# The second block's attention: the second pass of a score product over 128 rows in place of 64

## The chip, the cores and the metric

One core of a Trainium2 chip runs the whole program in one launch. The metric is the device time of that launch in microseconds (us), the median of several runs; smaller is better. The engines in the profile are PE (TensorE, with PEld for its weight loads), DVE (VectorE), ACT (ScalarE), POOL (GpSimd) and SP (SyncE), which here only issues DMAs.

## The reference, cut to what matters

The model is two blocks one behind the other, each of two layers, on 512 tokens of 1024 features in float32. The change lies in the second block's windowed attention: 16 query heads of 64 features, 4 heads of keys and values, each serving four query heads, in blocks of 128 tokens that see the block before, their own and the one behind.

```python
def windowed_gqa(q, k, v, rel_bias, sink):
    ...
    scores = jnp.einsum("bnqhgd,bnkhd->bhgnqk", qb, kb,
                        preferred_element_type=jnp.float32) * (HEAD_DIM ** -0.5)
    ...
    scores = jnp.where(valid, scores + bias, NEG_INF_2)
    sink_l = sink.astype(jnp.float32).reshape(N_KV_HEADS, G, 1, 1, 1)
    m = jnp.maximum(jnp.max(scores, axis=-1, keepdims=True), sink_l)
    p = jnp.exp(scores - m)
    denom = jnp.sum(p, axis=-1, keepdims=True) + jnp.exp(sink_l - m)
    p = (p / denom).astype(v.dtype)
    out = jnp.einsum("bhgnqk,bnkhd->bnqhgd", p, vb)
```

Beside it stand a convolution along the tokens, a pooling branch, gates, an output projection and a feed-forward part, as projections of 1024 (or 2816) features.

## The kernel before, in words

**Products in parts.** Every float32 value that goes through PE is split in a rounded part (`hi`, type float32r) and the rest (`lo`), so that two float32r tiles sum to it exactly. A projection is made of three passes for each 128 x 128 tile of weights (`mm3`, L259 to L261): `hi` by `hi`, `hi` by `lo`, `lo` by `hi`, all over 128 rows and mostly 512 columns, adding in one PSUM bank.

**Scores.** Queries and keys have 64 features, and the array has 128 rows. So `q_split` (L1280, L1281) puts both parts of a head's query on the 128 rows of one tile: for an even head the rounded part on rows 0 to 63 and the rest on rows 64 to 127, for an odd head the other way round. `k_evac` (L1261 to L1264) makes for each key head two tiles: one that holds the rounded part in both halves, and one that holds the rest in both halves (the second half of it is a copy by POOL, L1264). The product of a head and a block of 128 queries (`scores`) is then two passes in one bank: L1321 takes all 128 rows of the query against the rounded keys (both query parts by `hi`), L1322 the 64 rows with the query's rounded part against the keys' rests. The keys seen are 256 for the first and last block and 384 for the two between, so the passes have 256 or 384 columns. There are 16 heads x 4 blocks x 2 layers = 128 such products.

**What follows a product.** VectorE adds the bias and takes the maximum (L1324), forms the shift (L1328), ScalarE takes the exponential with its sum (L1329). When a head's four blocks are done, `scale` (L1338 to L1342, VectorE) divides by the sums, `turn` transposes 128 x 128 pieces on PE (L1352) and copies them out (L1355, VectorE and ScalarE in turns), `mix` multiplies them with the values (L1367, 64 columns of the array for each of two heads) and ScalarE copies the result out (L1370). PSUM has 8 banks, given out in turn.

**Order.** PE's order is fixed when the program is built. `weave` puts three streams together: the pairs' scores and scales (`sc`, 8 pairs of heads per layer), their turns and mixes (`tm`), and as filling the convolution branch's projections (`fill`, L1381 to L1396 on the other engines). An item has a cost (109 per 128 columns for a product) and due times behind the items that it needs, and the scores of a pair are spaced by 900 of the planner's units. The other engines' instructions are issued in the same order, with weights' splits (L1657, L1658) three chunks ahead. The bias of each pair is loaded by POOL's queue (L627) a pair ahead.

Of the kernel before, what the change touches and what calls it, by code (L numbers as in the profile page):

```python
# [49 lines left out]
# first block  # L50
# [11 lines left out]
# second block  # L62
# [6 lines left out]
# t5 bucket boundaries: bucket b begins at distance BOUND[b]  # L69
# [8 lines left out]
def shape_constants():  # L78
    """Constants that depend on the shapes alone."""
    hot1 = np.zeros((33, NT1), np.float32)  # L80
    for n in range(N0):
        j = 255 - n
        hot1[np.searchsorted(BOUND1, j, side="right") - 1 if 0 <= j <= 128 else 32, n] = 1.0
    for n in range(N1):
        j = 127 - n
        hot1[np.searchsorted(BOUND1, 4 * j, side="right") - 1 if j >= 0 else 32, N0 + n] = 1.0
        ok = j >= 0 and j % 4 == 0
        hot1[np.searchsorted(BOUND1, 4 * j, side="right") - 1 if ok else 32, N0 + N1 + n] = 1.0
    hot2 = np.zeros((33, NT2), np.float32)
    for n in range(NT2):  # L90
        rel = n - 255
        b = np.searchsorted(BOUND2, abs(rel), side="right") - 1 + (16 if rel > 0 else 0)
        hot2[b if abs(rel) <= 128 else 32, n] = 1.0
    # causal mask behind three blocks of zeros, edges of the pooling windows, rope's rows
    mask = np.zeros((P, 4 * P), np.float32)
    mask[:, 3 * P:] = np.where(np.arange(P)[None, :] <= np.arange(P)[:, None], 0.0, NEG)
    edge = np.ones((4, 16), np.float32)
    for g, w in enumerate(POOL_W):
        for t in range(w // 2):
            edge[g, t] = w / (t + w // 2)  # L100
        for t in range(S - w // 2 + 1, S):
            edge[g, 16 - (S - t)] = w / (S - t + w // 2)
    edge = np.broadcast_to(edge.reshape(1, 64), (P, 64))
    inv = (1.0 / np.power(np.float32(10000.0), np.arange(0, 32, 2, dtype=np.float32) / np.float32(32))).astype(np.float32)
    # rope's rows: 32 with the first halves of two heads, 32 with the second ones, and again for two more heads
    row = np.arange(P)
    freq = np.tile(inv, 8).reshape(P, 1)
    sign = np.where(row % 64 < 32, 1.0, -1.0).reshape(P, 1)
    parity = np.stack([row % 32 < 16, row % 32 >= 16], axis=1)
    small = np.ascontiguousarray(np.concatenate([mask, edge, freq, sign, parity], axis=1), np.float32)  # L110
    return np.concatenate([hot1, hot2], axis=1), small


class Weight:
    """One tile of weights, [128, n] as the host lays it out; split on the chip, or given to `use`."""
# [5 lines left out]
class Item:  # L121
    """A stretch of the tensor engine's work, with what follows from it on the other engines.

    after: items, each with the time that its results take to be ready behind it.
    """
# [14 lines left out]
class Order:  # L140
    """The tensor engine's order: streams of items woven so that what an item needs is ready."""
# [16 lines left out]
    def weave(self, *streams, hold=0):  # L158
        """The last stream is kept back by `hold`, to have some of it for the others' end."""
        total = [sum(i.cost for i in x) or 1 for x in streams]  # L160
        at, done = [0] * len(streams), [0.0] * (len(streams) - 1) + [float(hold)]
# [28 lines left out]
class Kernel:  # L190
# [31 lines left out]
    def held(self, n, dt=F32, tag=None):  # L222
        """A tile that the first block holds, or one of the second in its place."""
# [7 lines left out]
    def split(self, y, shift=None, factor=None):  # L231
        """y (+ shift, or * factor) as the sum of two float32r tiles: exact."""
        nc = self.nc
# [12 lines left out]
    def splits(self, ys):  # L246
        """Some tiles' splits, the engines taking turns."""
# [15 lines left out]
    def proj(self, get, cols, K, x, evac, m=P, step=8, grain=2, part=slice(0, S)):  # L263
        """Items for evac(W[:, cols].T @ X), X's tiles given by x() on use; or of X's columns `part`."""
# [20 lines left out]
    def proj_rows(self, get, cols, n, K, x, evac, step, blocks=(0, 1, 2, 3)):  # L285
        """Items for evac(i, (X.T @ W[:, cols])[rows of block i]); x() gives, by block, X's tiles."""
# [23 lines left out]
    def proj_wide(self, get, cols, x, evacs, part=slice(0, S), box=None):  # L310
        """Four projections at once, an item for every two of X's tiles; or the second of two parts, with the first's box."""
# [30 lines left out]
    def row_sums(self, acc, m=4):  # L342
        """Sums over the features, [token of block j, j]."""
# [5 lines left out]
    def root(self, ps, n, by=None, m=4):  # L349
        """1 / sqrt(mean + eps) of each token, the sums taken by a factor squared."""  # L350
# [9 lines left out]
        # a Newton step, as the table's root is short of float32  # L360
# [13 lines left out]
    def spread(self, dg, out=None):  # L374
        """The diagonals on all partitions."""
# [8 lines left out]
    def half_norm_items(self, l, half):  # L384
        """The first block's norm of half of the tokens: three items, then four for two feature tiles each."""
# [34 lines left out]
    def norm_items(self, acc, n, key):  # L420
        """Items that leave the tokens' factors under key, from the squares under acc."""
# [15 lines left out]
    def two_norms_items(self):  # L437
        """The same for a norm behind a norm: under r1 the first's factors, under r those of both."""
# [16 lines left out]
    def warm_sqrt(self, _):  # L455
        """The root's table, ahead of its use."""
# [8 lines left out]
    def setup(self):  # L465
        """What the first norm needs, and small constants."""
        nc, ap, st = self.nc, self.ap, self.st
        # silu(c) on all partitions, the first layer's input
# [15 lines left out]
        # keys of the first block; in the second, rows with zeros around the tokens and the pooling's partial sums  # L484
# [12 lines left out]
    def sigmoid2(self, ps):  # L497
        """tanh(x / 2), one short of twice the sigmoid: of the exponential's table."""
# [4 lines left out]
    def gated(self, out, s, y):  # L503
        """y by twice the sigmoid."""
        self.nc.vector.scalar_tensor_tensor(out, s, 1.0, y, ALU.add, ALU.mult)

    def warm(self, n):
        """Products of zeros: the array's clock stays up where it would wait for loads."""
# [27 lines left out]
    def setup_rope(self, _):  # L536
        """cos and the signed sin, for angles of any size."""
# [26 lines left out]
    def turned(self, ps, n):  # L564
        """Rows of rope, n of them, as the two terms of their sum."""
# [23 lines left out]
    def bias_tables(self, _):  # L589
        """Relative-position biases by distance, with masked distances in a row of their own."""  # L590
# [7 lines left out]
        # each table in 128 rows, to be read with a shift of one from row to row  # L598
# [11 lines left out]
    def load_bias1(self, hp):  # L610
        """[q, (head, g0's 256 keys | g1's 128 | g2's 128)] of two heads; g0's rows in order (t % 4, t // 4)."""
# [19 lines left out]
    def ada_weights(self, l):  # L631
# [3 lines left out]
        def use(raw, j):  # L635
            junk = self.t(BF16, [P, D])
            if l == 0 and j % 2 == 1 and j < 8:
                # beside the others, while there are many at once
# [12 lines left out]
    def ada_finish(self, l, ks):  # L651
        """Shift and scale of the feature tiles ks."""
# [17 lines left out]
    def first_layer(self, l):  # L670
# [20 lines left out]
        # -- latents and the shared rope key  # L691
# [15 lines left out]
        def kr_rope(_):  # L707
# [3 lines left out]
            # the keys' other parity is zero, as the rows of queries hold two heads  # L711
# [16 lines left out]
        # -- dilated: values  # L728
# [15 lines left out]
        # -- dilated: queries and keys of two heads  # L744
# [25 lines left out]
        # -- dilated attention of two heads  # L770
# [37 lines left out]
        # the groups' maxima and sums by token: g0's rows are (t % 4, t // 4) of block b, those of g1 and g2 t // 4 for t % 4  # L808
# [95 lines left out]
        else:  # L904
            # the first half of the tokens is ready, the second follows
# [62 lines left out]
    def first_rest(self, l, sc, tm, fill):  # L968
# [7 lines left out]
        # -- the dilated branch's way out  # L976
# [15 lines left out]
        # -- latent attention  # L992
# [88 lines left out]
        # what of it does not wait for the dilated branch's values goes beside that branch's end  # L1081
# [44 lines left out]
        # keys and queries of pair j + 2 take the places of those of pair j  # L1126
# [6 lines left out]
        # -- the latent branch's way out, the gates and the output projection  # L1133
# [20 lines left out]
        def x_load(_):  # L1154
            gate = self.mod[l][:, 16:24]
            # half of it, as what it gates is doubled
# [8 lines left out]
        def wo_evac(ps, f):  # L1165
            x = st["xr"][f]
            nc.vector.scalar_tensor_tensor(x, ps, self.mod[l][:, 16 + f:17 + f], x, ALU.mult, ALU.add)
            # the last norm's gains, and the next norm's, ahead of the tokens' factors
# [7 lines left out]
        def wo_half(ps, f, half):  # L1176
# [6 lines left out]
            # the squares one tile behind, so that they wait for nothing  # L1183
# [13 lines left out]
        if l + 1 < DEPTH:  # L1197
            # by halves of the tokens, so that the next norm of the first goes beside the second
# [14 lines left out]
    def ahead(self, x, gname, l, f):  # L1213
        """x with the next norm's gains, short of the tokens' factors."""
# [5 lines left out]
    def second_layer(self, l):  # L1220
# [8 lines left out]
        def norm(gname, wide, more):  # L1229
            """The norm's items, woven with those of a wide projection and others that go ahead of it."""  # L1230
# [21 lines left out]
        # -- keys (twice, for heads in the upper and the lower rows) and values  # L1252
        def k_evac(ps, i):
            # of each head the first part twice, [hi; hi], and the rest twice
# [20 lines left out]
        def q_split(y, j, scale):  # L1275
            """Of each head both parts on the 128 rows; the first where its keys are."""
# [20 lines left out]
        # -- attention  # L1297
# [3 lines left out]
        def scores(h, b):  # L1301
            j, h2 = h // 2, h % 2

            def fn(_):
# [12 lines left out]
                rs = slice(64 * h2, 64 * h2 + 64)  # L1317
# [4 lines left out]
                nc.tensor.matmul(ps[:, :n], lhsT=q[rs, qs], rhs=lo[rs, ks], start=False, stop=True)  # L1322
# [55 lines left out]
        # -- convolution along the tokens  # L1378
# [53 lines left out]
        # -- the branches' ways out, each with its gate  # L1432
# [100 lines left out]
        # -- feed-forward, in two halves of its width  # L1533
# [85 lines left out]
    def emit(self, items, chunks):  # L1619
        """Issue the items, with the weights' loads and splits ahead of them."""  # L1620
# [10 lines left out]
        def load(c):  # L1631
            off, ws = chunks[c]
            n = sum(w.n for w in ws)
            # the first loads have the places of later tiles too
# [41 lines left out]
# per-feature columns: name -> (first column, columns)  # L1676
# [64 lines left out]
```

## Time and profile before

| | |
|---|---|
| median of 3 runs | 3356.23 us (3355.78 to 3357.96) |
| profiled execution: span from its first to its last instruction | 3356.0 us; the profile shows no time outside it |
| PE busy | 3303.6 us, 98% |
| DVE, ACT, POOL busy | 54%, 38%, 12% |
| chain that ended last, by engine | PE 88%, DVE 4%, issue 3%, ACT 2% |
| DMA | 101 GB/s on average |

The table is read from the top: how long, who is busy, who is on the chain. A matmul's duration in this profile is longer than the time it takes from the stream (ends are modelled, and matmuls overlap), so the distance from one start to the next is what counts on PE. Times in a timeline are us from the start of the span.

### The profile page before, as it was taken

Reading aid. Unit: us, or ns where it says so; the run is one execution under the profiler, and the core shown is the slowest. Engines: PE = TensorE matmul, PEld = TensorE weight load, DVE = VectorE, ACT = ScalarE, POOL = GpSimd, SP = SyncE. Lnnn points to the kernel's source line nnn. Section 1 sums busy time; section 2 is a strip of 40 time slices with the busy share of each in tenths; the row PEclk is TensorE's granted clock in tenths of the full one; section 3 lists DMA queues with packets and bytes.
Section 4 is the critical chain, followed back from the end, with each engine's and each line's share of the span. In section 5 each row is a group of like instructions: output and inputs, shape, how many; then the busy total and the mean of one; then the engine's idle time right before and its main releaser. Section 6 shows DMA issues by size and latency. Waiting matters only on the chain.

```text
span 3356.0 us, 40708 instructions
## 1 busy us (share of the span) xinstructions
PE 3303.6 (98%) x15484; PEld 2625.9 (78%) x15488; DVE 1798.3 (54%) x3659; ACT 1275.2 (38%) x2432; POOL 396.9 (12%) x651
## 2 busy tenths in 40 slices
PE   8999999999999999999999999999999999999998
PEld 5878767799778677877688878888876788888886
DVE  7556776465446765576544555333666525463333
ACT  3344344343444443454433333223444423242222
POOL 3033301020122010200004110000000014000000
PEclk8999999999999999999999999999999999999999
DMA  6454531263221122332222332232322223322322
GB/s 221 138 160 150 124 88 67 82 214 126 82 70 56 53 74 76 124 115 77 73 88 80 109 113 101 88 104 82 127 90 71 70 89 99 125 88 91 110 89 69
DMA packets 104979, 340.20 MB, mean 101 GB/s; under 512 B 14116, under 2 KB 17236, under 8 KB 104784
## 3 DMA queue, kind: packets, MB, share of 16 engines
q1 hardware_dynamic: 94320, 309.90, 27.4%
q0 software_dynamic: 10464, 27.72, 3.3%
q8 instruction: 121, 1.98, 0.2%
q14 instruction: 74, 0.61, 0.1%
HBM read 329.04 MB, written 16.35 MB: 103 GB/s over the span
## 4 chain that ended last, share of the span: by engine, by line
PE 88%; DVE 4%; issue 3%; ACT 2%; DMA 1%; POOL 1%; DVEq 0%; SPq 0%; ACTq 0%; POOLq 0%
PE ps L259 25%; PE ps L260 24%; PE ps L261 24%; PE ps L1034 2%; PE ps L1322 1%; PE ps L1367 1%; PE ps L1352 1%; PE ps L1072 1%; PE ps L302 1%; PE ps L303 1%; PE ps L304 1%; PE ps L1059 1%; DMA rows<-dt 1%; PE ps L888 1%; PE ps L790 1%
## 5 line engine op out<-in xcount | busy, mean ns | idle before, releaser
L259 PE MATMUL ps<-t,hi 128*128 128x512 f32 (+1 forms) x3904 | 1553.2, 398 | 6.8 <-ACT t L239 3.9
L260 PE MATMUL ps<-t,hi 128*128 128x512 f32 (+1 forms) x3904 | 1504.2, 385 | 0.9 <-DVE t L240 0.7
L261 PE MATMUL ps<-t,lo 128*128 128x512 f32 (+1 forms) x3904 | 1503.7, 385 | 0.0
L1658 DVE TENSOR_TENSOR lo<-raw,hi 128x1024 fp32r<-128x1024 f32 (+5 forms) x562 | 666.5, 1188 | 732.9 <-ACT hi L1657 732.4
L259 PEld LDWEIGHTS ps<-t,hi 128*128 128x128 f32 x3904 | 735.0, 188 | 184.9 <-issue 20.3
L261 PEld LDWEIGHTS ps<-t,lo 128*128 128x128 f32 x3904 | 735.1, 188 | 148.3
L260 PEld LDWEIGHTS ps<-t,hi 128*128 128x128 f32 x3904 | 735.9, 189 | 145.3 <-issue 6.7
L1657 ACT CAST hi<-raw 128x1024 fp32r<-128x1024 f32 (+6 forms) x566 | 551.5, 977 | 238.4 <-PE ps L260 156.3
L239 ACT CAST t<-t 128x512 fp32r<-128x512 f32 x154 | 91.0, 619 | 376.6 <-DVE t L1559 174.6
L240 DVE TENSOR_TENSOR t<-t,t 128x512 fp32r<-128x512 f32 x154 | 106.7, 716 | 105.9 <-ACT t L239 105.9
L805 ACT ACTIVATE p<-p,sm 128x128 f32<-128x128 f32 (+1 forms) x192 | 80.1, 418 | 142.7 <-DVE sm L802 142.6
L1329 ACT ACTIVATE p<-p,sm 128x256 f32<-128x256 f32 (+1 forms) x128 | 72.1, 563 | 162.1 <-DVE sm L1328 161.1
L1040 ACT ACTIVATE p<-p,sm 128x128 f32<-128x128 f32 (+3 forms) x128 | 71.9, 562 | 157.8 <-DVE sm L1039 156.8
L302 PE MATMUL ps<-hi,t 128*128 128x512 f32 (+1 forms) x272 | 105.2, 387 | 12.2 <-ACT t L242 11.7
L303 PE MATMUL ps<-hi,t 128*128 128x512 f32 (+1 forms) x272 | 102.6, 377 | 0.6 <-DVE t L243 0.6
L304 PE MATMUL ps<-lo,t 128*128 128x512 f32 (+1 forms) x272 | 101.7, 374 | 0.0
L1435 ACT ACTIVATE t<-ps 128x512 f32<-128x512 f32 x48 | 28.7, 598 | 171.3 <-PE ps L261 171.3
L1462 POOL TENSOR_TENSOR c<-c 128x527 f32<-128x527 f32 (+3 forms) x40 | 51.8, 1294 | 346.1 <-ACT c L1458 344.1
L1034 PE MATMUL ps<-c,t 128*128 128x128 f32 (+3 forms) x256 | 89.7, 439 | 0.4 <-DVE t L999 0.4
L1002 POOL TENSOR_TENSOR t<-t,t 64x512 f32<-64x512 f32 x32 | 42.3, 1336 | 358.6 <-DVE t L571 237.2
L302 PEld LDWEIGHTS ps<-hi,t 128*128 128x128 f32 x272 | 68.0, 250 | 19.4 <-ACT t L242 14.1
L1559 DVE TENSOR_TENSOR t<-ps,t 128x512 f32<-128x512 f32 x38 | 26.3, 692 | 101.4 <-PE ps L261 101.4
(229 smaller groups left out, 2850.1 us busy)
## 6 DMA issues: line engine op xcount, KB each, us to landing
raw<-in_w_dram SPq DMA_DIRECT2D x512, 512.0 KB, 3.3
raw<-in_w_dram SPq DMA_DIRECT2D x32, 384.0 KB, 3.0
raw<-in_w_dram SPq DMA_DIRECT2D x32, 320.0 KB, 2.8
xd<-t SPq DMA_DIRECT2D x24, 256.0 KB, 4.8
t<-xd POOLq DMA_DIRECT2D x24, 256.0 KB, 5.3
bias<-rows POOLq DMA_DIRECT2D x32, 192.0 KB, 2.8
rows<-dt POOLq DMA_DIRECT2D x1, 4088.0 KB, 38.8
raw<-in_w_dram SPq DMA_DIRECT2D x10, 256.0 KB, 2.6
```

The costliest lines, as they stand in the source:

```text
L239: nc.scalar.copy(hi, y)
L240: nc.vector.tensor_tensor(lo, y, hi.bitcast(F32), ALU.subtract)
L259: mm(out, lhsT=w[0], rhs=x[0], start=start, stop=False)
L260: mm(out, lhsT=w[0], rhs=x[1], start=False, stop=False)
L261: mm(out, lhsT=w[1], rhs=x[0], start=False, stop=stop)
L302: mm(ps, lhsT=xh, rhs=hi[:, s], start=k == 0, stop=False)
L303: mm(ps, lhsT=xl, rhs=hi[:, s], start=False, stop=False)
L304: mm(ps, lhsT=xh, rhs=lo[:, s], start=False, stop=k == kt - 1)
L805: nc.scalar.activation(pr[:, s], pr[:, s], AF.Exp, bias=nm[:, g, h2, b:b + 1], accum_out=ml[:, 1, g, h2, b:b + 1])
L1034: nc.tensor.matmul(ps[:, :n], lhsT=st["q", h][:, b * P:(b + 1) * P], rhs=self.kh[h % 4][:, :n], start=True, stop=True)
L1657: nc.scalar.copy(hi[:, :n], src[:, :n])
L1658: (nc.gpsimd if chunks[c][1][0].aside else nc.vector).tensor_tensor(lo[:, :n], src[:, :n], hi[:, :n].bitcast(F32), ALU.subtract)
```

## The change

The second pass takes all 128 rows: both parts of the query against the keys' rests, which lie on both halves. The result gets one term more, rest by rest. The slice of rows is dropped; the number, order and planned cost of the instructions stay. The other lines of the diff only take comments and docstrings out, one line for one line, so that line numbers behind the dropped slice are smaller by one.

```diff
@@ -1314,12 +1314,11 @@
                 pr, sm = st["p", h], st["st", h]
                 n = (HI[b] - LO[b]) * P
                 o = 384 * h2 + (LO[b] - b + 1) * P
-                rs = slice(64 * h2, 64 * h2 + 64)
                 ps = self.ps()
                 q, (hi, lo) = st["q", h], st["k", h // 4]
                 qs, ks = slice(b * P, (b + 1) * P), slice(LO[b] * P, HI[b] * P)
                 nc.tensor.matmul(ps[:, :n], lhsT=q[:, qs], rhs=hi[:, ks], start=True, stop=False)
-                nc.tensor.matmul(ps[:, :n], lhsT=q[rs, qs], rhs=lo[rs, ks], start=False, stop=True)
+                nc.tensor.matmul(ps[:, :n], lhsT=q[:, qs], rhs=lo[:, ks], start=False, stop=True)
```

## Rows read from the trace of the kernel before

**Rows 1.** The page's part 1: busy us, share of the span, instructions.

```profile
PE 3303.6 (98%) x15484; PEld 2625.9 (78%) x15488; DVE 1798.3 (54%) x3659; ACT 1275.2 (38%) x2432; POOL 396.9 (12%) x651
```

**Rows 2.** Stretches, both layers' attention: length, busy PE, PEld, DVE, ACT, POOL, clock, DMA.

```profile
1450.00:1691.00 241.00, 241.00 (x1095) 169.85 (x1094) 151.01 (x400) 107.30 (x244) 7.52 (x14) 1.00 0.26 87
2419.00:2660.00 241.00, 241.00 (x1095) 169.88 (x1094) 150.77 (x400) 107.52 (x244) 6.44 (x12) 1.00 0.25 84
```

**Rows 3.** The chain that ended last, from 1447 to 1690, by line.

```profile
by line: PE ps L259 26.8%; PE ps L261 21.8%; PE ps L260 21.7%; PE ps L1322 9.0%; PE ps L1352 8.4%; PE ps L1367 8.3%; PE ps L1321 4.1%
```

**Rows 4.** Line L1322: durations in ns, forms; idle before it (us, times).

```profile
L1322 PE MATMUL ps<-held,t x96: 379/410/444, 1451.2 to 2585.4; 64*128 64x256 f32 x48, 64*128 64x384 f32 x48
...
L1322 PE MATMUL ps<-t,t x32: 379/410/443, 1622.9 to 2645.5; 64*128 64x256 f32 x16, 64*128 64x384 f32 x16
...
  issue: 27.8, 106
```

**Rows 5.** Timeline around the first product: start, length, engine, line, [idle before].

```profile
1450.33 0.39 PE L259 MATMUL ps<-t,hi 128*128 128x512 f32 x1
1450.33 0.19 PEld L260 LDWEIGHTS ps<-t,hi 128*128 128x128 f32 x1
1450.56 0.39 PE L260 MATMUL ps<-t,hi 128*128 128x512 f32 x1
...
1451.01 0.28 PE L1321 MATMUL ps<-t,t 128*128 128x256 f32 x1
...
1451.21 0.18 PEld L1322 LDWEIGHTS ps<-held,t 64*128 64x128 f32 x1 [0.24 <-issue]
1451.21 0.38 PE L1322 MATMUL ps<-held,t 64*128 64x256 f32 x1
...
1451.52 0.50 PE L259 MATMUL ps<-t,hi 128*128 128x512 f32 x1
...
1451.86 0.40 PE L260 MATMUL ps<-t,hi 128*128 128x512 f32 x1
```

**Rows 6.** Timeline of passes over 128 rows and 256 columns.

```profile
1439.74 0.28 PE L302 MATMUL ps<-hi,t 128*128 128x256 f32 x1
1439.86 0.28 PE L303 MATMUL ps<-hi,t 128*128 128x256 f32 x1
```

**Rows 7.** Timeline, a product over 384 columns and the second pass behind it.

```profile
1455.02 0.33 PE L1321 MATMUL ps<-t,t 128*128 128x384 f32 x1
...
1455.99 0.40 PE L260 MATMUL ps<-t,hi 128*128 128x512 f32 x1
```

**Rows 8.** Timeline, a product that a mix follows.

```profile
1520.80 0.38 PE L1322 MATMUL ps<-held,t 64*128 64x256 f32 x1
...
1521.11 0.65 PE L1367 MATMUL ps<-t,t 128*64 128x256 f32 x4
```

**Rows 9.** Timeline of POOL, the last of the keys' copies.

```profile
1433.03 0.61 POOL L1264 CAST t<-t 64x512 fp32r<-64x512 f32 x1 [0.74 <-DVE t L1262]
```

**Rows 10.** Timeline, from the first product to the first turn, both layers.

```profile
1461.14 0.42 DVE L1324 CUSTOM_DVE_ANT_0 p<-ps,bias 128x256 f32<-128x256 f32 x1
...
1477.17 1.28 DVE L1342 TENSOR_SCALAR p<-p,sm 128x256 f32<-128x256 f32 x4
...
1478.41 0.33 PE L1321 MATMUL ps<-t,t 128*128 128x384 f32 x1
...
1480.53 0.38 PE L1352 MATMUL ps<-c,p 128*128 128x128 f32 x2
...
2445.76 1.28 DVE L1342 TENSOR_SCALAR p<-p,sm 128x256 f32<-128x256 f32 x4
...
2449.31 0.39 PE L1352 MATMUL ps<-c,p 128*128 128x128 f32 x2
```

**Rows 11.** Waits from 1450 to 1691: us in total, times, longest.

```profile
DVE t L1355 <- PE ps L1352: 14.3, 13, 3.2
...
DVE p L1324 <- PE ps L1322: 12.1, 11, 2.8
```

## The prediction

> **What bounds the kernel now.** I read first the page's busy shares [rows 1]: the tensor engine is busy for 98% of the span, VectorE, the next, for 54%. A busy tensor engine may still hold bubbles, as the ends of its matmuls are modelled, so the second view is the table of stretches, for the two stretches in which the second block's attention runs, one per layer [rows 2]: in 241 us each PE has no idle time, the weight loads fill 170 us, VectorE 151 us, ScalarE 107 us, and the granted clock is 1.00, the upper level of 2.4 GHz. The chain inside the first of them [rows 3] is PE alone, and the pass that the change touches, L1322, holds 9.0% of it although it does little of the work. So here the end is set by how soon one matmul may start behind the other, and start-to-start times are to be read, not durations. The third view is that line's own summary [rows 4]: 96 and 32, so 128 second passes, half over 256 and half over 384 columns; 27.8 us of idle time stand before them in 106 cases under "issue", which means that nothing the profile shows was awaited. The fourth is the timeline around one score product.
>
> **What one score product costs.** Among full passes, L260 starts 0.23 us behind L259, and its load (all 128 rows) begins while L259 streams [rows 5]. With 256 columns, passes over 128 rows follow each other at 0.12 us, each with weights of its own [rows 6]. The score product over 256 columns departs from that: from L1321 at 1451.01 to the 64-row L1322 it takes 0.20, from there to the next projection's L259 0.31, and from that to L260 0.34, though L259 has 512 columns like any other; 0.85 in all [rows 5]. L1322's load comes after 0.24 of idle time and starts with its matmul, where L260's ran ahead of it. So going to the 64 rows costs about 0.1 and coming back about 0.3, at two places: before L259, and behind it. With 384 columns, it is 0.97 from L1321 to L260 [rows 7].
>
> **The change part by part.** Nothing is added or removed in count: one matmul with one weight load stays one, in the same place of the order; the planner's costs (109 per 128 columns) are untouched, so no DMA, split or evacuation moves in any queue. The stationary and the moving side of the second pass grow from 64 to 128 rows, of tiles that are whole already.
>
> *The second pass.* As a 128-row pass of the same type as L1321 it should stand in the stream like any other. 256 columns: 0.12 + 0.12 + 0.23 = 0.47 in place of 0.85, which saves 0.38. For 384 columns the trace has no such pass in a stream; it lies between the spacing of 256 (0.12) and of 512 columns (0.23). I take the middle, 0.175: 0.175 + 0.175 + 0.23 = 0.58 in place of 0.97 saves 0.39. The ends are 0.97 - 0.47 = 0.50 and 0.97 - 0.69 = 0.28. Sum: 64 x 0.38 + 64 x 0.39 = 49.3 us, between 42.2 and 56.3. From below, that the bigger pass costs what the smaller one did, or that its stalls are of another cause, the bound is no gain; it is a rival.
>
> *Weighed against the trace.* In [rows 5] the 128-row load of L260 begins at 1450.33, in the moment when the 128-row L259 starts streaming, and costs the stream nothing. The Trainium skill ("TensorE: Matmul & The Clock Gate", The mechanism) says that a weight load overlaps a matmul in flight only when their row groups differ. By that rule the load of a second pass over all rows would stand as bare behind L1321 as now and the change would bring nothing, 3356 us; by the row, the 49.3 us above. The trace speaks against the rule for this stream, and I go by the row.
>
> *Four products* in the two layers are followed not by a projection but by L1367, which writes 64 columns of the array [rows 8]; at the near edge L1367 stands 0.31 behind L1322, and it stays a change of shape. I count half of the saving there as kept: 4 x 0.2 = 0.8 less, 48.5 us.
>
> *A wait that may be added.* The second pass now reads both halves of the keys' rests; one half is a copy that POOL makes (L1264). The last of the first layer's begins at 1433.03 and takes 0.61 [rows 9]; the first product is at 1451.01 [rows 5], 17.4 us later. Later heads use the same tiles, so all are written by then. Cost nothing; hidden behind that stretch of projections.
>
> *What is late next.* PE comes earlier by about 0.385 us per product, the other engines do not. The first turn (L1352) of a layer's first pair of heads needs the scaled probabilities (L1342) that end at 1477.17 + 1.28 = 1478.45; PE reaches it at 1480.53 [rows 10], a slack of 2.1 us. VectorE is behind there (the first product's sums, at 1451 on PE, are taken up at 1461.14 [rows 10]), so it does not come earlier with PE. Eleven products stand before that turn, from 1451.01 [rows 5] to 1478.41 [rows 10]: PE will be 4.2 us early, and waits 2.1. In the second layer L1342 ends at 2445.76 + 1.28 = 2447.04 and the turn is at 2449.31 [rows 10]: slack 2.3, wait 1.9. Together 4.0 us are given back. Behind it VectorE catches up: it waits 12.1 us on L1322 and 14.3 us on L1352 in the first layer's stretch [rows 11], 26.4 us against some 24 us that the layer is to lose. So later pairs should cost nothing, though not with much to spare; if that cover fails the first rival comes.
>
> Sum: 48.5 - 4.0 = 44.5 us. The profiled execution shows no time around its span of 3356.0 us; the median of the runs is 0.2 us above it. 3356.2 - 44.5 = **3312 us** (1.3% faster).
>
> **The rivals.**
> 1. *VectorE takes over.* Its slack in the stage is about as large as the gain [rows 11], and ScalarE and VectorE wait for each other there. If PE is held up by 2.1 us at the first turn of each of the 16 pairs and not only of two, 33.6 us are lost: 3356.2 - 48.5 + 33.6 = 3341; with half of the pairs 3324. For it: the first pair's small slack [rows 10]. Against it: VectorE has 90 us without work in each stretch [rows 2]. 15%.
> 2. *Only the gap before the load goes.* Then the gain is the 27.8 us of "issue" [rows 4], 3328 us: the late L260 behind the next L259 would have to be of another cause. Against it: that 0.34 stands nowhere in the plain stream [rows 5]. 6%.
> 3. *The rows are not the cause*, but, say, the second pass adding to the bank that the first has just written, or loads that do not overlap between passes on the same rows (the skill's rule above). The change does nothing: 3356 us. Against it: L260 adds to L259's bank at 0.23 [rows 5]. 4%.
> 4. *Slower: the wait for POOL's copy.* Its place is the first product of each layer's pairs; all of PE's stream is queued behind it, so its price is its whole length. It costs something only if the copies end more than 17.4 us later against PE than now, and makes the kernel slower only beyond 17.4 + 24 = 41 us; at 45 us it would be 4 us per layer, 3364 us. Before them POOL has little to do, and they take 0.61 each [rows 9]. 2%.
>
> **How the numbers follow.** Forecast 73% (the gain less what VectorE takes back, 34 to 52 us: 3304 to 3322), VectorE 15% (3324 to 3341), half the stall 6% (3328), nothing 4%, slower 2%. The low end comes from 384 columns at the spacing of 256 with the same give-back (56.3 - 4.8 = 51.5 us: 3305, and one below); the high end takes in rival 2 and the milder half of rival 1: 3304 to 3330. Within 0.2% (6.7 us) counts as the same, about what a measurement of this kernel can tell from no change. Faster: 73 + 15 + 6 = 94%; same 4%; slower 2%.
>
> **What would show it.** In the profile after (line numbers behind the edit fall by one): the second pass has the form 128x256 and 128x384, its load starts ahead of its matmul, and its "issue" row is gone; L260 stands 0.23 behind the L259 that follows; L1321 to L260 takes 0.47 or about 0.58. PE shows a wait of about 2 us for VectorE at the first pair's turns, once per layer, and none in the other pairs. I am wrong in the size if the 384-column spacing is near an end; wrong in what follows if PE's idle before turns or mixes totals over 10 us; wrong in the mechanism if the spacings around the second pass stay.

## The result, and the profile after

The changed kernel takes 3314.69 us (median of 4 runs, 3314.45 to 3316.44) against 3356.01 us before: 0.9878 of the time, 95% interval 0.9865 to 0.9890. That is 41 us less; 44.5 were forecast, and the stated range holds it. On another chip the same kernel, once more, took 3314.80 us. Line numbers behind the edit are smaller by one: L1320 and L1321 are now the two passes.

The first thing to look at is the new second pass: its rows by line, of the changed kernel (durations in ns: least, median, greatest; then the forms).

```profile
L1321 PEld LDWEIGHTS ps<-held,t x96: 187/188/192, 1450.9 to 2547.6; 128*128 128x128 f32 x96
L1321 PE MATMUL ps<-held,t x96: 277/308/340, 1451.1 to 2547.7; 128*128 128x256 f32 x48, 128*128 128x384 f32 x48
```

The shape is 128 by 128, and the "issue" row that stood there before ([rows 4], 27.8 us) is gone. The timeline around the first product, and around the third, which has 384 columns, answers to [rows 5] and [rows 7].

```profile
1450.94 0.28 PE L1320 MATMUL ps<-t,t 128*128 128x256 f32 x1
1450.94 0.19 PEld L1321 LDWEIGHTS ps<-held,t 128*128 128x128 f32 x1
1451.05 0.28 PE L1321 MATMUL ps<-held,t 128*128 128x256 f32 x1
1451.17 0.39 PE L259 MATMUL ps<-t,hi 128*128 128x512 f32 x1
1451.41 0.39 PE L260 MATMUL ps<-t,hi 128*128 128x512 f32 x1
...
1454.14 0.33 PE L1320 MATMUL ps<-t,t 128*128 128x384 f32 x1
1454.31 0.34 PE L1321 MATMUL ps<-held,t 128*128 128x384 f32 x1
1454.48 0.39 PE L259 MATMUL ps<-t,hi 128*128 128x512 f32 x1
1454.71 0.40 PE L260 MATMUL ps<-t,hi 128*128 128x512 f32 x1
```

From the first pass to the next projection's L260 it is now 0.47 in place of 0.85, and 0.57 in place of 0.97. The load of L1321 begins with the streaming of L1320, on the same 128 rows, and is hidden. All 64 products of a layer stand in the stream this way; for the two that a mix follows, L1366 comes 0.21 behind L1321 in place of 0.31, so 0.19 is saved and not 0.39. A layer should gain 32 x 0.38 + 32 x 0.40 - 2 x 0.2 = 24.6 us.

How much of it is kept is read between two fixed points of PE's order, the first product and the last mix of each layer. These are rows of PE's timeline, first of the kernel before:

```profile
1689.35 1.55 PE L1367 MATMUL ps<-t,t 128*64 128x384 f32 x8
...
2419.78 0.28 PE L1321 MATMUL ps<-t,t 128*128 128x256 f32 x1
...
2658.15 1.51 PE L1367 MATMUL ps<-t,t 128*64 128x384 f32 x8
```

and of the changed one (its first product of the first layer is the first row of the fence above):

```profile
1667.98 1.55 PE L1366 MATMUL ps<-t,t 128*64 128x384 f32 x8
...
2397.03 0.28 PE L1320 MATMUL ps<-t,t 128*128 128x256 f32 x1
...
2613.90 1.51 PE L1366 MATMUL ps<-t,t 128*64 128x384 f32 x8
```

The first layer's stage shrinks from 238.34 us (1451.01 in [rows 5] to 1689.35) to 217.04, by 21.3; the second's from 238.37 to 216.87, by 21.5. So each gives back 3.1 to 3.3 us of its 24.6. Together the stages gain 42.8 us, the span 43.3 (3356.0 to 3312.7).

The 3.3 us are waits of PE that the stage did not have before; its table of stretches shows some 2 us in which PE is idle, in each layer (columns as in [rows 2]; the ends of matmuls are modelled, so the idle time shown is less than what the spacings lose).

```profile
1450.00:1669.00 219.00, 216.93 (x1092) 167.74 (x1091) 149.52 (x400) 106.28 (x243) 7.51 (x14) 1.00 0.28 95
2397.00:2616.00 219.00, 217.08 (x1092) 167.58 (x1091) 148.49 (x400) 106.82 (x245) 6.43 (x12) 1.00 0.27 92
```

PE's timeline names the places; all lie in the first 50 us, the larger ones in the first 35. In brackets stands the idle time and what ended it.

```profile
1465.07 0.47 PE L259 MATMUL ps<-t,hi 128*128 128x512 f32 x1 [0.87 <-DVE sm L1323]
...
1477.53 0.65 PE L1351 MATMUL ps<-c,p 128*128 128x128 f32 x2 [0.18 <-DVE p L1341]
...
1482.11 0.44 PE L1351 MATMUL ps<-c,p 128*128 128x128 f32 x2 [0.48 <-DVE sm L1323]
1482.70 0.44 PE L1351 MATMUL ps<-c,p 128*128 128x128 f32 x2 [0.15 <-DVE sm L1323]
1483.42 0.44 PE L1351 MATMUL ps<-c,p 128*128 128x128 f32 x2 [0.28 <-DVE sm L1323]
```

By the distance of starts beyond what the same pair of passes usually takes, the wait at 1465 costs 1.0 us, that for scaled probabilities (L1341) 0.6, the three at 1482 and 1483 cost 1.4 together, and one more at 1495 (not shown) 0.3: 3.3 us. (The passes right behind a wait also start late, by 0.4 us in all; small gains elsewhere balance that.) What is telling is the releaser: L259 multiplies weights by the normed input, which VectorE's maximum of a product (L1323) has no part in. What it can wait for is the PSUM bank of a product whose maximum is not yet taken. A count bears this out. If PE's order is followed from the first product, and each of the 8 banks is handed out again in the order in which the program gives them back, L259 at 1465.07 gets the bank of the second product, whose maximum is there at 1464.92. The three turns get the banks of the ninth to the eleventh product, whose maxima are there at 1482.05, 1482.64 and 1483.36: each turn starts 0.06 us later. The wait at 1495 falls on the fifteenth product's bank in the same way, and the second layer gives the same five.

### The profile page after: what moved, and what is told of

The parts are those of the page before. It is cut to its first block, busy times and chain, and to the rows that moved or that the text cites. A ratio compares the mean times of both kernels' runs of the same rounds, so it can differ in the third digit from the quotient of the medians.

```text
span 3312.7 us, 40712 instructions
## 1 busy us (share of the span) xinstructions
PE 3259.3 (98%) x15488; PEld 2622.2 (79%) x15488; DVE 1794.1 (54%) x3659; ACT 1273.7 (38%) x2432; POOL 397.2 (12%) x651
## 4 chain that ended last, share of the span: by engine, by line
PE 85%; DVE 6%; issue 3%; ACT 3%; DMA 1%; POOL 1%; DVEq 0%; SPq 0%; ACTq 0%; POOLq 0%
PE ps L259 24%; PE ps L260 24%; PE ps L261 24%; PE ps L1034 1%; DVE lo L1657 1%; PE ps L1366 1%; PE ps L1072 1%; PE ps L1351 1%; PE ps L1059 1%; DMA rows<-dt 1%; PE ps L888 1%; PE ps L790 1%; PE ps L302 1%; PE ps L303 1%; PE ps L304 1%
## 5 line engine op out<-in xcount | busy, mean ns | idle before, releaser
L259 PE MATMUL ps<-t,hi 128*128 128x512 f32 (+1 forms) x3904 | 1538.5, 394 | 8.0 <-ACT t L239 3.9
L260 PE MATMUL ps<-t,hi 128*128 128x512 f32 (+1 forms) x3904 | 1502.4, 385 | 0.9 <-DVE t L240 0.9
L259 PEld LDWEIGHTS ps<-t,hi 128*128 128x128 f32 x3904 | 734.3, 188 | 168.6 <-issue 11.2
L260 PEld LDWEIGHTS ps<-t,hi 128*128 128x128 f32 x3904 | 734.8, 188 | 144.7 <-issue 6.7
L239 ACT CAST t<-t 128x512 fp32r<-128x512 f32 x154 | 91.0, 619 | 376.6 <-DVE t L1558 174.6
L302 PEld LDWEIGHTS ps<-hi,t 128*128 128x128 f32 x272 | 68.2, 251 | 15.7 <-ACT t L242 10.3
```

Source lines behind the costliest of these rows:

```text
L239: nc.scalar.copy(hi, y)
L259: mm(out, lhsT=w[0], rhs=x[0], start=start, stop=False)
L260: mm(out, lhsT=w[0], rhs=x[1], start=False, stop=False)
L302: mm(ps, lhsT=xh, rhs=hi[:, s], start=k == 0, stop=False)
```

## The experiments

Twelve runs followed. The first four, of one execution each, ask what the change of rows costs; the others ask where 3.3 us per layer stay.

**The 64-row pass twice** (of the kernel before):

```diff
-                nc.tensor.matmul(ps[:, :n], lhsT=q[rs, qs], rhs=lo[rs, ks], start=False, stop=True)
+                nc.tensor.matmul(ps[:, :n], lhsT=q[rs, qs], rhs=lo[rs, ks], start=False, stop=False)
+                nc.tensor.matmul(ps[:, :n], lhsT=q[rs, qs], rhs=lo[rs, ks], start=False, stop=True)
```

> The kernel before, with the 64-row second pass issued twice in a row, on the same rows (the keys' rests count twice). Theory A: the cost lies in changing between 128 and 64 rows, 0.39 us per product for going and coming back; a further pass inside the 64-row shape then costs its columns alone, 0.11 us (256) or 0.16 us (384), 128 of them 17 us: 3373 us, and between the two 64-row passes the spacing is 0.11 or 0.16. Rival B: a 64-row pass is slow in itself, wherever it stands; each further one loses its 0.39 us again, 17 + 50 us: 3423 us. Rival C: a load is never hidden behind a pass on the same rows; 0.1 us more for each, 3386 us.

Measured: 3377.90 us, beside 3358.39 of the kernel before on that chip: 19.5 us more for 128 passes, 0.15 each. In the traces the two stages from first product to last mix hold 18.7 us of it. Theory A's sum holds, B's and C's do not. A's spacing does not hold. The timeline of the first product:

```profile
1451.31 0.28 PE L1321 MATMUL ps<-t,t 128*128 128x256 f32 x1
1451.51 0.18 PEld L1322 LDWEIGHTS ps<-held,t 64*128 64x128 f32 x1 [0.24 <-issue]
1451.52 0.38 PE L1322 MATMUL ps<-held,t 64*128 64x256 f32 x1
1451.62 0.19 PEld L1323 LDWEIGHTS ps<-held,t 64*128 64x128 f32 x1
1451.74 0.28 PE L1323 MATMUL ps<-held,t 64*128 64x256 f32 x1
1451.94 0.50 PE L259 MATMUL ps<-t,hi 128*128 128x512 f32 x1
1452.28 0.39 PE L260 MATMUL ps<-t,hi 128*128 128x512 f32 x1
```

From the first to the second 64-row pass it is 0.22 and not 0.11, and from there to L259 0.20, where it was 0.31 behind the only one. So the first 64-row pass itself starts late behind its recorded start, as L259 does on the way back. Each change of shape costs the same on both ways: 0.09 us ahead of the first pass of the new shape and 0.11 behind it, 0.2 in all. Inside the shape the second pass's load starts 0.1 ahead of its matmul and stalls nothing.

**The passes exchanged** (of the kernel before):

```diff
-                nc.tensor.matmul(ps[:, :n], lhsT=q[:, qs], rhs=hi[:, ks], start=True, stop=False)
-                nc.tensor.matmul(ps[:, :n], lhsT=q[rs, qs], rhs=lo[rs, ks], start=False, stop=True)
+                nc.tensor.matmul(ps[:, :n], lhsT=q[rs, qs], rhs=lo[rs, ks], start=True, stop=False)
+                nc.tensor.matmul(ps[:, :n], lhsT=q[:, qs], rhs=hi[:, ks], start=False, stop=True)
```

> The kernel before, with the two passes of each product exchanged: the 64-row pass first, the 128-row pass behind it. Theory A (changing shape costs): the sum stays, 3356 us within 5, but the places move: about 0.09 us more than the plain 0.23 before the 64-row pass, 0.31 (256 columns) or 0.37 (384) from it to the 128-row pass, which now takes the late start (0.1 more than plain behind it), and the next projection's L259 to L260 is back at 0.23. Rival B (the second pass adds to the bank that the first has just written): the stall stays between first and second pass and before L259, whichever pass comes first, and L259 to L260 stays at 0.34.

Measured: 3356.26 us. The stalls moved with the 64-row pass, as theory A has it:

```profile
1449.80 0.39 PE L261 MATMUL ps<-t,lo 128*128 128x512 f32 x1
1450.12 0.38 PE L1321 MATMUL ps<-held,t 64*128 64x256 f32 x1
1450.43 0.39 PE L1322 MATMUL ps<-t,t 128*128 128x256 f32 x1
1450.65 0.39 PE L259 MATMUL ps<-t,hi 128*128 128x512 f32 x1
1450.89 0.39 PE L260 MATMUL ps<-t,hi 128*128 128x512 f32 x1
```

0.32 before the 64-row pass (0.23 is plain), 0.31 from it to the 128-row pass, 0.22 behind that (0.12 is plain), and L259 to L260 plain again. Writing into the bank just written is not the cause.

**96 rows** (of the changed kernel):

```diff
-                nc.tensor.matmul(ps[:, :n], lhsT=q[:, qs], rhs=lo[:, ks], start=False, stop=True)
+                nc.tensor.matmul(ps[:, :n], lhsT=q[0:96, qs], rhs=lo[0:96, ks], start=False, stop=True)
```

> The changed kernel, with the second pass over rows 0 to 95 (so a part of the rests of the products is left out in odd heads, and a part of rest by rest in even ones). Theory A: what counts is whether the pass leaves the array in its undivided shape; 96 rows fit no smaller shape, so it runs as 128 rows: 3315 us within 3, spacings 0.11 and 0.12. Rival D: any pass with fewer rows than the one before it stalls: 3356 us.

Measured: 3315.75 us; the timeline has no stall:

```profile
1450.82 0.28 PE L1320 MATMUL ps<-t,t 128*128 128x256 f32 x1
1450.93 0.28 PE L1321 MATMUL ps<-held,t 96*128 96x256 f32 x1
1451.05 0.40 PE L259 MATMUL ps<-t,hi 128*128 128x512 f32 x1
1451.28 0.40 PE L260 MATMUL ps<-t,hi 128*128 128x512 f32 x1
```

A pass with fewer rows than its neighbours does not stall for that; one with 64 does. That fits a change of the array's shape and not the count of rows (32 rows were not tried).

**The 128-row pass twice** (of the changed kernel, the same edit as in the first experiment).

> The changed kernel, with its 128-row second pass issued twice in a row (the rests count twice). It prices a 128-row pass by itself. Theory A: 0.12 us (256 columns) and 0.17 us (384), 128 of them 18.6 us, of which some 3 us fall into PE's waits at the head of each layer: 3328 to 3334 us. Rival: the rule that a load overlaps only a pass on other rows; each load of 0.19 us stands bare, 128 x 0.3 to 0.36 us = 42 us: 3357 us.

Measured: 3322.93 us, 8 us more than the changed kernel; less than either theory. The spacings are theory A's: 0.12 for each further pass over 256 columns, 0.18 over 384.

```profile
1448.82 0.28 PE L1320 MATMUL ps<-t,t 128*128 128x256 f32 x1
1448.93 0.28 PE L1321 MATMUL ps<-held,t 128*128 128x256 f32 x1
1449.05 0.28 PE L1322 MATMUL ps<-held,t 128*128 128x256 f32 x1
```

The passes cost 9.4 us per layer by them; each layer's stage grew by 7.2, as PE comes later to its waits and 2.2 us of these go. That makes 14 us; the other 6 were gained outside the stages. Of these, 2.9 us are a wait for ScalarE between the layers (L259 behind L239), which the changed kernel has and this one has not; why, was not pursued. Another 2.1 us lie ahead of the first product (1448.82 against 1450.94). That product begins anywhere from 1448.67 to 1450.94 in the three profiled executions of the changed kernel, so these 2.1 us say nothing of the edit.

**Four chunks of weights split by POOL** (of the changed kernel), and once more on another chip beside the changed kernel:

```diff
             conv += self.proj(w_in, rng(B_B + f * P, P), D, H, lambda ps, f=f: b_evac(ps, f))
+        for it in conv[0:13:4]:
+            it.w[0].aside = True
```

> The changed kernel, with the lower parts of four chunks of the convolution branch's weights (those at the head of each layer) split by POOL, which is idle there, and not by VectorE. It takes some 4.9 us of VectorE's work away ahead of the first pair's scores. Theory E: the 3.3 us that PE loses in each layer's first 50 us are waits for PSUM banks and scaled probabilities that VectorE gives back late, because it comes behind from the layer's head; with 4.9 us less ahead of them they go: 3315 - 6 = 3309 us. Rival F: these waits hang on the exchange between ScalarE and VectorE inside the softmax, not on the backlog: 3315 us, no change. Rival G: POOL takes 2.5 us for a chunk and the projections wait for it: over 3315 us.

> The four splits by POOL alone, once more, beside the changed kernel on the same chip: 2.2 us less in each layer by the first run's trace, so 3310 to 3311 us if only PE's waits count; 3308 if the whole difference of the medians, 7 us, comes back.

Measured: 3307.71 and 3308.23 us. Beside them on the same chips the changed program took 3314.36 (the run told of next) and 3314.80, so 6.6 us less by the medians; as a ratio to the kernel before 0.9862 (0.9849 to 0.9876), where the changed kernel beside it has 0.9875 (0.9859 to 0.9890). These intervals overlap, and the changed kernel's fastest run there, 3307.67 us, lies among those with the splits. What the traces show is the stage from first product to last mix: 2.2 to 2.3 us shorter in each layer, in both runs. The other 2 us lie outside, are no more than what two executions of one program differ by there, and stay open. Of PE's waits in the first layer's stage two are left, one of 0.3 us by the starts at 1491.90 and this one (second run):

```profile
1479.44 0.44 PE L1351 MATMUL ps<-c,p 128*128 128x128 f32 x2 [0.28 <-DVE sm L1323]
```

Theory E's number holds, but its reason does not. VectorE takes up the first product no sooner behind PE than without the edit: 10.3 us (1459.50 against 1449.22) in place of 10.1 (1461.07 against 1450.94), as its own operations took longer beside POOL's splits (last section). What is gone is a split that stood between the first and the second maximum. In the changed kernel VectorE waits there for ScalarE's rounded part, and the second maximum begins 3.43 us behind the first:

```profile
1463.36 1.23 DVE L1657 TENSOR_TENSOR lo<-raw,hi 128x1024 fp32r<-128x1024 f32 x1 [1.61 <-ACT hi L1656]
1464.50 0.42 DVE L1323 CUSTOM_DVE_ANT_0 p<-ps,bias 128x256 f32<-128x256 f32 x1
```

With the splits by POOL it begins 0.60 behind:

```profile
1459.50 0.42 DVE L1323 CUSTOM_DVE_ANT_0 p<-ps,bias 128x256 f32<-128x256 f32 x1
...
1460.10 0.41 DVE L1323 CUSTOM_DVE_ANT_0 p<-ps,bias 128x256 f32<-128x256 f32 x1
```

The 2.83 us between are the wait of 1.61 and the 1.22 of work. Theory F's exchange has a part in it: ScalarE makes that rounded part at 1462.29, behind the first product's exponential at 1461.79, which waited for VectorE's shift. So PE's first wait for a bank hangs on this one split in VectorE's queue: without it the wait is gone, though VectorE enters the layer as late as before. What the other three splits bring these rows do not show; a run that moves that one alone is missing.

**The first pair later, three times** (of the changed kernel). The first edit, `BQ + 8000` for the first pair, changed nothing in the order of any engine, since the due time had long passed at that place; it is a repeat of the changed kernel.

> The changed kernel, with the first pair's scores of each layer put 8000 planner units later, behind further projections. Theory E (VectorE's backlog at the head): VectorE has caught up by then, the 3.3 us of PE's waits per layer go: 3309 us if the filling lasts to the end, with some of it lost if the last pair is left with less beside it (each layer's last turns and mixes then wait): 3309 to 3316. Rival F (exchange between ScalarE and VectorE): the waits move with the scores: 3315 us or more.

Measured: 3314.36 us; it tells nothing of either theory. The other two hold the first pair behind two projections, and behind one:

```diff
             s[0].after.append((qp[j][-1], BQ))
+            if j == 0:
+                s[0].after.append((conv[7], 0))     # conv[3]: one projection
```

> The changed kernel, with the first pair's scores of each layer held behind the first two projections of the convolution branch (some 11 us of PE); the order of what follows closes up behind them. Theory E (PE's 3.3 us of waits per layer come from VectorE's backlog of about 10 us at the layer's head): the backlog is gone when the scores begin, the waits in the first 50 us go, 3309 us; but the products of the second pair then follow each other at 0.9 us, so some waits for VectorE may come back there. Rival F (the exchange between ScalarE and VectorE inside the softmax holds PE up, wherever the first pair stands): the waits move along, 3315 us or more.

> The same with one projection in place of two (5.5 us). Theory E: VectorE is still some 5 us behind when the scores begin, about as far as PE's banks bear without a wait; the waits in the first 50 us shrink from 3.3 to under 1 us per layer, 3310 to 3312 us. Rival F: 3315 us, waits as before the shift.

Measured: 3323.46 and 3322.25 us (0.9904 and 0.9897 of the kernel before): slower than the change alone (0.9878) by the medians, though the intervals, 0.9888 to 0.9921 and 0.9882 to 0.9912, overlap a little with that of the change, 0.9865 to 0.9890, and no changed kernel ran beside them. It goes against both numbers of theory E. Where the first pair stood no wait for VectorE's maxima is left, but the pairs behind stand closer together, and there a new one arises. With one projection, beside a smaller one of 0.65 us at 1517.74:

```profile
1485.75 0.69 PE L1320 MATMUL ps<-t,t 128*128 128x384 f32 x1 [2.73 <-DVE sm L1323]
```

with two projections, one of 3.12 us at 1492. The waiter is the first pass of a product, whose query and keys were written long before: it waits for the bank that another product still holds. This is the plainest row for banks; by the count told of above it gets the eleventh product's, whose maximum is there at 1485.69. Around the stage (1445 to 1675, 2392 to 2627) PE is idle for 4.4 us per layer in place of 2.0; that is some 5 of the 8 us, and the rest was not found.

**One bank for a pair's 256-column products**, alone and with the splits by POOL (of the changed kernel):

```diff
-                ps = self.ps()
+                if b in (0, 3):
+                    if h2 == 0:
+                        st["both"] = self.ps()
+                    ps = st["both"][:, 256 * h2:256 * h2 + 256]
+                else:
+                    ps = self.ps()
```

> The changed kernel; the two products of a pair over 256 columns (first and last block) share one PSUM bank, 256 columns each, so a pair takes 6 banks in place of 8. VectorE's work and the order stay. Theory E1 (PE's waits at the head of a layer are for banks): of the 3.3 us per layer, 2.7 us are waits for a bank (1.0 before a projection, 1.4 before turns, 0.3 later); most of it goes: 3310 to 3312 us, and the wait of L259 at 1465 is gone. Rival E2 (the waits are for scaled probabilities or maxima): 3315 us, same waits.

> The changed kernel with both: shared banks for 256-column products, and four chunks of weights at the head of each layer split by POOL. Theory E: both act on the same 3.3 us per layer, so the gains don't add up: at most 6.6 us in all, 3308 us, about what the splits by POOL alone give. Rival: they act on different waits and add up below 3306 us.

Measured: 3341.94 and 3342.24 us: a miss, 27 us slower than the change alone. The edit adds a wait that I had not seen: the second product of the pair is put behind VectorE's reading of the first, as both lie in one tile; PE stands still until that reading, which begins at 1456.65, is done.

```profile
1457.14 0.58 PE L1325 MATMUL ps<-t,t 128*128 128x256 f32 x1 [8.85 <-DVE sm L1328]
```

So it does not test what fewer banks would bring. It does show how far VectorE is behind at the layer's head: 8.9 us.

**The changed kernel again**, on one chip with the two kernels that share a bank and the repeat of the splits by POOL:

> The changed kernel once more, unchanged, beside the three that follow: 3315 us within 2, as every theory has it. It is the base that the others are read against.

Measured: 3314.80 us.

## Why the prediction was right, and where it was not

- **The second pass in the stream: right.** 0.47 us for 256 columns as forecast, 0.57 for 384 where 0.58 was the middle taken; the first passes follow at 0.17. With the four products before a mix (0.19 saved, half was counted) the gross gain is 2 x 24.6 = 49.2 us, where 48.5 was forecast.
- **What causes it: right in the sum, wrong in the places.** The step "going to the 64 rows costs about 0.1 and coming back about 0.3" took recorded starts for the streaming. Both ways cost 0.2, as the exchanged and the doubled pass show.
- **The rule weighed against the trace.** The Trainium skill ("TensorE: Matmul & The Clock Gate", The mechanism) says that a load overlaps a matmul in flight only when the row groups differ; the same section also lets a load run ahead when it goes to the background weight buffer, which the prediction left out. The trace of the changed kernel disagrees with the first as a rule for all loads: L1321's load runs beside L1320 on the same 128 rows, and the further 128-row pass costs 0.12. No run here shows which buffer a load writes.
- **POOL's copy: right.** The first L1321 follows its L1320 by 0.11.
- **What is late next: right engine and place, wrong in the instruction and the size.** The step named the first turn's scaled probabilities and 2.1 and 1.9 us per layer. They cost 0.6 us: the first turn needs two of L1341's four segments, not all of them (its transposes start at 1477.53 and 1477.85, 0.06 behind the first and the second segment), so the slack was larger than worked out; and PE had lost 1.0 of its lead at 1465. The PSUM banks that VectorE frees late were not in the sum, and cost 2.7 us. The layers gave back 3.3 and 3.1 us, 6.4 in place of 4.0. That the sum came so near is luck: a wait that was too large stood in it for others that were missing.
- **VectorE as the new bound (rival 1): no.** From the third pair on PE gains its 0.4 us with every product; no wait was added behind the first 50 us. The idle time of VectorE covered it.
- **The base.** "No time around the span" was wrong: the profiled run after took 3314.45 us with a span of 3312.7, so 1.8 us lie outside. The spans differ by 43.3 us, the medians by 41.3: with the same 1.8 us around it, the execution profiled before took about 3357.8 us, some 1.8 above the median.
- **Open:** that the 2.7 us are banks rests on the waiting instructions' operands, on the run with the later first pair and on the count of banks above, which fits every one of these waits; a run with banks alone changed is missing.

## What to carry to other kernels

In this kernel a pass over 64 rows among passes over 128 costs more than one over all of them: 0.2 us to go and 0.2 to come back, while the further rows cost nothing. Fill the rows with something useful, or gather the small passes. When PE comes earlier, look for what the slower engine has still to give back, banks as well as data: here 6 of 49 us went there, and four splits on an idle engine brought 4.5 of them back in the traces. Look also for what stands between two small operations in the slower engine's queue: one split that waited for a third engine held the second maximum up by 2.8 us.

## What was not expected of the hardware

- 96 rows run in the stream of 128-row passes without a stall, 64 do not (0.11 and 0.12 against 0.20 and 0.31).
- VectorE slows beside POOL's splits: in the kernel with splits by POOL (second run), two normed tiles (L461) take 3.56 us beside a split of 2.57; the two at 1440.95, with no split beside them, take 1.41. The queries' rests (L1281) take 2.60 and 2.67 beside the next two splits, in place of 1.40. Both runs show it in both layers. The gain of that kernel is net of this. VectorE's row, and POOL's:

```profile
1443.65 3.56 DVE L461 SCALAR_TENSOR_TENSOR t<-t,c,t 128x512 f32<-128x512 f32 x2
```

```profile
1444.10 2.57 POOL L1659 TENSOR_TENSOR lo<-raw,hi 128x1024 fp32r<-128x1024 f32 x1 [12.25 <-ACT hi L1658]
```
